# A mixed MLA and mLSTM trunk: decay rows by DRAM transfers, first loads reordered, output factors by token

## The chip, the cores and the metric

One NeuronCore of a Trainium2 chip runs the kernel. The metric is the device time of one execution in microseconds; lower is better. The engines are named as in the profile: PE (TensorE, matmul), DVE (VectorE), ACT (ScalarE), POOL (GpSimd) and SP (SyncE, which here only issues transfers).

## What is computed

Two layers over 512 tokens of width 1024, float32. Each layer adds half a SwiGLU, a token mixer and half a SwiGLU to the residual, each behind an RMS norm; layer 0 mixes with multi-head latent attention, layer 1 with the mLSTM, which the change is about:

```python
def mlstm(h, w_in, b_if, conv_w, conv_b, out_norm, w_o):
    p = h @ w_in
    qk = silu(causal_depthwise_conv(p[..., :QK], conv_w, conv_b))
    ...
    i_pre = gates[..., :H]
    log_f = log_sigmoid(gates[..., H:])
    hid = mlstm_chunkwise(q, k, v, i_pre, log_f)
    hid = hid * rsqrt(mean(hid * hid, axis=-1) + RMS_EPS)
    hid = hid.reshape(B, S, V) * out_norm * sigmoid(o)
    return hid @ w_o
```

Within it, a head's scores are weighted by `exp(D - m_t)`, where `D[t, s] = F[t] - F[s] + i[s]` for s up to t, `F` is the running sum of `log_f` and `m_t` the running maximum that stabilises the exponent. The output of a token is `num / max(|den|, exp(-m_t))`, and then it is normalised over the 128 channels of its head. There are 8 heads.

## The kernel before, in words

Activations lie transposed: channels on the 128 partitions, the 512 tokens along the free axis. A float32 operand is split into a high part (`hi`, rounded by ACT: the CAST rows) and the rest (`lo`, made by DVE), and a product is three matmuls of 128 x 512: hi hi, hi lo, lo hi (`mm3`). Weights come as chunks of 128 x 1024: SP (some on POOL) loads `raw`, ACT casts `whi`, DVE subtracts `wlo`; there are three buffers of each, and `weights()` has the split of the chunk two ahead issued. `defer(n, step)` runs a step when the nth next chunk is asked for. The program is written in this order, but the order within each engine is set by a scheduler that weighs what is ready when; the lists in the section on the change are its outcome.

The program runs the phases f0, a, f1, f2, m, f3 (four feed-forward parts, the attention `a`, the mLSTM `m`).

*Start.* `begin` warms PE with 36 small matmuls, loads the vectors `par`, the constants `cst`, the eight tiles `x` of the residual and the first two chunks of gate and up weights in quarters, and splits them. `stats` squares the x tiles into `acc`; `rstd` sums `acc` over the partitions on PE (`st`), adds a constant on DVE (`ms`), raises to the power -0.5 on POOL (`r`), and `spread(r)` brings it back along the partitions on PE (`bc`).

*mLSTM.* `log_forget` and `stabilise` (run during the first half of `values`) make rows on 8 partitions, one for a head: `m` (the running maximum), `fl` (the running sum within a tile of 128 tokens), `z`, `em` = exp(-m), and `lf` = fl - m. `columns` turns `z` and its shifts to tokens on partitions (bank `cb`, columns `cols`). `decay(h)` needs row h of `lf` on all 128 partitions: before, `spread(rows, h)` did it with a matmul of `rows` (the split of `lf`) against a selector column (L1133), into a PSUM bank. ACT then takes ten exponentials of 128 x 128 (`dw`, L1155), four of which read `dg`, the row with the causal mask added by DVE. The scores `s` times `dw` give the weights `ws[h]`; their sums over s are kept too. `mix(h)` multiplies them with the values (`num`), and adds, in the bank `rows` of `acc`, the sums over s to row h and, through `squares`, the sum of num squared to row 32 + h.

`factors(half, squares)` makes the output factors of four heads. Before, it worked on rows of 512 tokens, 8 partitions: `Abs` and a copy on ACT, three operations on DVE (L1223 to L1225), then PE turned the result to tokens on partitions (`ab`, L1049 by way of `turn`), ACT copied it (`fc`), POOL took `pow(-0.5)` (`fp`), PE turned it back (`fb`), and the split `frows` was spread again for `gated(h)`. It is a generator: its three steps are deferred so that they fall between weight chunks. In the first half they run before the chunk of `conv(3)` and before the first and third chunk of `values(1)`; in the second half between the output projections `out(0, 1)` to `out(0, 3)`, whose matmuls are named `y`.

Of the kernel before, what the change touches and what calls it, by code (L numbers as in the profile page):

```python
# [26 lines left out]
F32 = mybir.dt.float32  # L27
# [39 lines left out]
class Trunk:  # L67
# [68 lines left out]
    def load_pieces(self):  # L136

        name, pieces, pool, plus = self.loads[len(self.loaded)]

        ap = self.row(*name)  # L140
        raw = self.duo(pool, F32) if pool else self.wp.tile([P, W], F32, name="raw", tag="raw")
        self.loaded.append(raw)
        for a, b in pieces:
            queue = self.nc.gpsimd if plus and name[0] == "wgs" else self.nc.sync
            queue.dma_start(out=raw[:, a:b], in_=ap[:, a:b])
            yield
        if plus:
            self.nc.gpsimd.dma_start(out=raw, in_=self.row(*plus), accum_op=ALU.add)  # L148
# [185 lines left out]
    def begin(self, gcol):  # L334
        nc = self.nc
        self.used = 0
        self.later = []
        self.mhalf = self.const.tile([P, NT], F32, name="mhalf")
        nc.vector.memset(self.mhalf, -0.5)

        warm = self.small.tile([P, P], BF16, name="warm", tag="warm", bufs=1)
        nc.vector.memset(warm, 0.0)
        nc.scalar.copy(out=warm[:, 0:1], in_=warm[:, 1:2])
        idle = self.ps2.tile([P, T], F32, name="idle", tag="st")
        for i in range(WARM):
            nc.tensor.matmul(idle[:, 0:P], warm, warm, start=True, stop=True)
        self.par = self.const.tile([P, V_END], F32, name="par")
        nc.sync.dma_start(out=self.par, in_=self.t["vecs"])
        cst = self.const.tile([P, self.t["cst"].shape[1]], F32, name="cst")
        self.ident = cst[:, 0:P]  # L350
        self.mask = cst[:, P:2 * P]
        self.maskT = cst[:, 2 * P:3 * P]
        self.invf, self.sign, self.one = (cst[:, 3 * P + i:3 * P + i + 1] for i in range(3))
        self.sel = cst[:, 3 * P + 3:3 * P + 11]
        self.norm_begin(gcol)
        quarters = [(k * 256, k * 256 + 256) for k in range(4)]
        for i in range(2):
            self.loads[i] = self.loads[i][0], quarters, None, None
        for i in range(2):
            load, split = self.load_pieces(), self.split_pieces(quarters, False)  # L360
            for k in range(4):
                d = 4 * i + k
                nc.sync.dma_start(out=self.x[d], in_=self.t["xT"][d * P:(d + 1) * P, :])
                next(load)
                self.norm_split(d)
                next(split)
            list(load), list(split)
            if i == 0:
                nc.sync.dma_start(out=cst, in_=self.t["cst"])
        self.todo = list(range(ND))  # L370

    def constants(self):
# [614 lines left out]
    def mlstm(self, next_gain):  # L987
# [63 lines left out]
        def small(name, n=32):  # L1051
            return self.small.tile([P, n], F32, name=name, tag=name, bufs=1)
# [28 lines left out]
            v.scalar_tensor_tensor(out=f, in0=pl, scalar=-2.0, in1=f, op0=ALU.mult, op1=ALU.add)  # L1081

        m, fl = self.t512("m"), self.t512("fl")
        rows, frows = self.pair()
        em = self.small.tile([P, T], F32, name="em", tag="rb", bufs=2)

        def stabilise():
            lb = self.bank("lb")
            for j in range(NT):
                turn(lb, j * P, f[:, 8 * j:8 * j + 8])  # L1090
            lf = self.t512("lf")
            s.copy(out=lf[g8], in_=lb[g8])

            ones = self.t512("first")
            v.tensor_tensor_scan(m[g8], lf[g8], z[g8], 0.0, ALU.add, ALU.max)
            nc.gpsimd.memset(ones[g8], 1.0)
            nc.gpsimd.memset(tiles(ones[g8])[:, :, 0:1], 0.0)
            v.tensor_tensor_scan(fl[g8], ones[g8], lf[g8], 0.0, ALU.mult, ALU.add)

            for a in (rows, frows):  # L1100
                nc.gpsimd.memset(a.bitcast(F32), 0.0)
            v.tensor_tensor(out=lf[g8], in0=fl[g8], in1=m[g8], op=ALU.subtract)
            self.split_to((rows[g8], rows[32:40]), lf[g8])
            v.tensor_tensor(out=z[g8], in0=z[g8], in1=fl[g8], op=ALU.subtract)
            v.tensor_scalar(em[g8], m[g8], -1.0, 43.0, ALU.mult, ALU.min)
            s.activation(em[g8], em[g8], AF.Exp)
# [2 lines left out]
        self.defer(4, stabilise)  # L1109
        values(0)  # L1110
        place = [(0, 0), (1, 0), (2, 0), (1, 384)]
        ws, sums, nums, ys, sg, sg_of, acc, which = {}, {}, {}, {}, {}, {}, {}, {}
        cols = small("cols", 80)

        def columns():

            cb = self.bank("cb")
            for i in range(NT):
                src = z[g8, i * P:(i + 1) * P]
                bt = self.t512("bt") if i < NT - 1 else None  # L1120
                for j in range(i, NT):
# [3 lines left out]
                        src = dst  # L1125
                    which[i, j] = 8 * len(which)
                    turn(cb, which[i, j], src)
            s.copy(out=cols, in_=cb[:, 0:80])


        def spread(rows, h):
            b = self.ps2.tile([P, T], F32, name="spread", tag="st")
            nc.tensor.matmul(b, self.selr[:, h:h + 1].broadcast_to([P, P]), rows, start=True, stop=True)  # L1133
            return b

        def decay(h):
            q, k = qk[h // 2], qk[4 + h // 2][h % 2]
            br = spread(rows, h)
            banks = [self.bank("s") for _ in range(3)]
            for i in range(NT):  # L1140
                b, c = place[i]
# [73 lines left out]
        def factors(half, squares):  # L1215

            for f in squares:
                f()
            a, n = self.t512("a"), self.t512("n")
            s.activation(a[g8], acc["rows"][g8], AF.Abs)  # L1220
            sq = self.t512("sq")
            s.copy(out=sq[g8], in_=acc["rows"][32:40])
            v.tensor_tensor(out=a[g8], in0=a[g8], in1=em[g8], op=ALU.max)  # L1223
            v.scalar_tensor_tensor(out=n[g8], in0=a[g8], scalar=EPS, in1=a[g8], op0=ALU.mult, op1=ALU.mult)
            v.scalar_tensor_tensor(out=a[g8], in0=sq[g8], scalar=1.0 / P, in1=n[g8],  # L1225
                                   op0=ALU.mult, op1=ALU.add)
            yield
            ab = self.bank("ab")
            for j in range(NT):
                turn(ab, 8 * j, a[g8, j * P:(j + 1) * P])  # L1230
            fc, fp = small("fc", 16), small("fp", 16)
            s.copy(out=tiles(fc), in_=tiles(ab[:, 0:32])[:, :, 4 * half:4 * half + 4])
            nc.gpsimd.tensor_tensor(out=fp, in0=fc, in1=self.mhalf[:, 0:1].broadcast_to([P, 16]), op=ALU.pow)
            yield
            fb = self.bank("fb")
            for j in range(NT):
                turn(fb, j * P, fp[:, 4 * j:4 * j + 4])
            self.split_to((frows[0:4], frows[32:36]), fb[0:4])
            yield
# [16 lines left out]

        gate(0)
        columns()
        gate(1)
        decay(0)  # L1260
        conv(1)
        decay(1)
        for p in range(3):
            a, b = 2 * p, 2 * p + 1
            conv(p + 5) if p < 2 else gate(5)
            gate(a + 2)
            pending = [mix(a), mix(b)]
            if p == 1:
                steps = factors(0, pending)
                for i in (1, 2, 4):  # L1270
                    self.defer(i, lambda: next(steps))
                conv(3)
                values(1)
# [218 lines left out]
```

## Time and profile before

| | |
|---|---|
| median of 3 runs | 1839.35 us (1837.66 to 1840.27) |
| the profiled execution | 1836.03 us |
| its span in the trace | 1834.3 us |
| PE busy | 1808.8 us, 99% |
| DVE, ACT, POOL busy | 1458.8, 938.6, 181.3 us |
| mLSTM phase | from about 1239 to 1490 us of the span |

Busy shares are averages over stages with different limits. Matmuls are pipelined and their ends modelled, so PE's pace is read from the distance between their starts. A row of the timeline gives the start, the busy time, the engine, line, operation and tiles of a run of like instructions, and in brackets how long the engine had been idle and what ended that.

### The profile page before, as it was taken

Reading aid. Unit: us, or ns where it says so; the run is one execution under the profiler, and the core shown is the slowest. Engines: PE = TensorE matmul, PEld = TensorE weight load, DVE = VectorE, ACT = ScalarE, POOL = GpSimd, SP = SyncE. Lnnn points to the kernel's source line nnn. Section 1 sums busy time; section 2 is a strip of 40 time slices with the busy share of each in tenths; the row PEclk is TensorE's granted clock in tenths of the full one; section 3 lists DMA queues with packets and bytes.
Section 4 is the critical chain, followed back from the end, with each engine's and each line's share of the span. In section 5 each row is a group of like instructions: output and inputs, shape, how many; then the busy total and the mean of one; then the engine's idle time right before and its main releaser. Section 6 shows DMA issues by size and latency. Waiting matters only on the chain.

```text
span 1834.3 us, 30137 instructions
## 1 busy us (share of the span) xinstructions
PE 1808.8 (99%) x12258; PEld 1662.9 (91%) x12258; DVE 1458.8 (80%) x1934; ACT 938.6 (51%) x1350; POOL 181.3 (10%) x233
## 2 busy tenths in 40 slices
PE   9999999999999999999999999999999999999997
PEld 7999989978887999989989999997877779999897
DVE  7887898777767887877797879778878778788875
ACT  5544535567543444534544444455767544445344
POOL 1210001000001210000021000100010012100011
PEclk9999999999999999999999999999999999999999
DMA  8875376421126865466589356633212268753763
GB/s 273 241 221 152 120 189 150 138 75 64 47 94 196 234 190 149 137 184 152 196 217 265 105 162 190 167 106 112 81 63 70 74 186 249 202 151 117 188 150 104
DMA packets 80860, 282.45 MB, mean 154 GB/s; under 512 B 9105, under 2 KB 12305, under 8 KB 80721
## 3 DMA queue, kind: packets, MB, share of 16 engines
q1 hardware_dynamic: 52416, 179.06, 28.2%
q0 software_dynamic: 27728, 100.94, 25.4%
q8 instruction: 96, 1.57, 0.3%
q10 hardware_dynamic: 576, 0.52, 0.1%
q14 instruction: 44, 0.35, 0.1%
HBM read 270.01 MB, written 10.49 MB: 153 GB/s over the span
## 4 chain that ended last, share of the span: by engine, by line
PE 72%; issue 16%; DVE 4%; DMA 3%; ACT 3%; POOL 1%; SPq 0%; POOLq 0%; DVEq 0%; ACTq 0%
PE pz L481 4%; PE pw L479 4%; PE pz L479 4%; PE pw L480 4%; PE pz L480 4%; PE pw L481 4%; PE px L479 4%; PE px L480 4%; PE px L481 4%; PE y L217 3%; PE y L218 3%; PE y L219 3%; DMA sum<-in_wds 2%; PE py L479 2%; PE py L480 2%
## 5 line engine op out<-in xcount | busy, mean ns | idle before, releaser
L185 ACT CAST whi<-raw 128x1024 fp32r<-128x1024 f32 (+1 forms) x278 | 284.4, 1024 | 388.9 <-issue 120.7
L186 DVE TENSOR_TENSOR wlo<-raw,whi 128x1024 fp32r<-128x1024 f32 (+1 forms) x278 | 330.3, 1191 | 110.4 <-ACT whi L185 110.2
L185 ACT CAST whi<-sum 128x1024 fp32r<-128x1024 f32 x208 | 217.4, 1048 | 290.9 <-PE pz L480 72.9
L186 DVE TENSOR_TENSOR wlo<-sum,whi 128x1024 fp32r<-128x1024 f32 x208 | 253.1, 1221 | 67.4 <-ACT whi L185 67.2
L173 DVE TENSOR_TENSOR sum<-raw,sum 128x1024 f32<-128x1024 f32 x88 | 107.3, 1219 | 15.3 <-DMA raw<-in_wgs 14.6
L148 POOL DMA_DIRECT2D sum<-in_wgs x72 | 63.4, 880 | 290.1 <-DMA sum<-in_wgs 273.3
L481 PE MATMUL pz<-b5h,wlo 128*128 128x256 f32 x288 | 81.2, 282 | 0.6 <-DVE wlo L186 0.6
L479 PE MATMUL pz<-b5h,whi 128*128 128x256 f32 x288 | 81.3, 282 | 0.0
L479 PE MATMUL px<-b1h,whi 128*128 128x256 f32 x288 | 81.3, 282 | 0.0
L479 PE MATMUL pw<-b7h,whi 128*128 128x256 f32 x288 | 81.3, 282 | 0.0
L479 PE MATMUL px<-b2h,whi 128*128 128x256 f32 x288 | 81.3, 282 | 0.0
L480 PE MATMUL pw<-b4l,whi 128*128 128x256 f32 x288 | 81.3, 282 | 0.0
L480 PE MATMUL py<-b6l,whi 128*128 128x256 f32 x288 | 81.3, 282 | 0.0
L480 PE MATMUL px<-b1l,whi 128*128 128x256 f32 x288 | 81.3, 282 | 0.0
L479 PE MATMUL py<-b6h,whi 128*128 128x256 f32 x288 | 81.3, 282 | 0.0
L479 PE MATMUL pw<-b4h,whi 128*128 128x256 f32 x288 | 81.3, 282 | 0.0
L479 PE MATMUL pz<-b3h,whi 128*128 128x256 f32 x288 | 81.3, 282 | 0.0
L480 PE MATMUL pz<-b3l,whi 128*128 128x256 f32 x288 | 81.3, 282 | 0.0
L480 PE MATMUL pw<-b7l,whi 128*128 128x256 f32 x288 | 81.3, 282 | 0.0
L480 PE MATMUL px<-b2l,whi 128*128 128x256 f32 x288 | 81.3, 282 | 0.0
L480 PE MATMUL pz<-b5l,whi 128*128 128x256 f32 x288 | 81.3, 282 | 0.0
L481 PE MATMUL pz<-b3h,wlo 128*128 128x256 f32 x288 | 81.2, 282 | 0.0
(423 smaller groups left out, 6201.1 us busy)
## 6 DMA issues: line engine op xcount, KB each, us to landing
sum<-in_wgs POOLq DMA_DIRECT2D x144, 512.0 KB, 6.7
raw<-in_wgs SPq DMA_DIRECT2D x108, 512.0 KB, 5.6
sum<-in_wds POOLq DMA_DIRECT2D x48, 512.0 KB, 6.3
raw<-in_wds SPq DMA_DIRECT2D x48, 512.0 KB, 3.3
sum<-in_wds SPq DMA_DIRECT2D x32, 512.0 KB, 4.4
raw<-in_wgc SPq DMA_DIRECT2D x30, 512.0 KB, 3.6
raw<-in_wdn SPq DMA_DIRECT2D x24, 512.0 KB, 3.7
away<-x SPq DMA_DIRECT2D x16, 512.0 KB, 3.8
```

What stands on the lines that cost most here:

```text
L148: self.nc.gpsimd.dma_start(out=raw, in_=self.row(*plus), accum_op=ALU.add)
L173: self.nc.vector.tensor_tensor(out=t, in0=a, in1=b, op=ALU.add)
L185: self.nc.scalar.copy(out=hi[:, a:b], in_=raw[:, a:b])
L186: self.nc.vector.tensor_tensor(out=lo[:, a:b], in0=raw[:, a:b], in1=hi[:, a:b].bitcast(F32), op=ALU.subtract)
L217: mm(out, lhs[0], rhs[0], start=start, stop=False)
L218: mm(out, lhs[0], rhs[1], start=False, stop=False)
L219: mm(out, lhs[1], rhs[0], start=False, stop=stop)
L479: mm(out, wh, bh[:, b], start=first and e + k == 0, stop=False, skip_group_check=True)
L480: mm(out, wh, bl[:, b], start=False, stop=False, skip_group_check=True)
L481: mm(out, wl, bh[:, b], start=False, stop=last and e + k == 4, skip_group_check=True)
```

## The change

It has three parts. (1) `stabilise` writes `lf` to a DRAM tile `away`, and `apart(p)` brings two rows of it back, each repeated along the 128 partitions by a transfer that POOL issues; `decay` reads that SBUF tile, and the spread by matmul and the split of `lf` go. (2) `begin` issues the loads of the x tiles and the weight quarters alternately and `cst` after them; four memsets of one column on the x tiles stand ahead. (3) `factors` copies rows 0 to 39 of the bank at once (`both`), turns them, and does the arithmetic with tokens on partitions, in 16 columns; `columns` turns `em` too, so that its columns are at hand; the steps of the first half are deferred to the chunks 2, 3 and 5 instead of 1, 2 and 4. The line of `queue` in `load_pieces` is moved out of a loop and issues the same.

```diff
--- before.py
+++ after.py
@@ -136,12 +136,11 @@
     def load_pieces(self):
 
         name, pieces, pool, plus = self.loads[len(self.loaded)]
-
+        queue = self.nc.gpsimd if plus and name[0] == "wgs" else self.nc.sync
         ap = self.row(*name)
         raw = self.duo(pool, F32) if pool else self.wp.tile([P, W], F32, name="raw", tag="raw")
         self.loaded.append(raw)
         for a, b in pieces:
-            queue = self.nc.gpsimd if plus and name[0] == "wgs" else self.nc.sync
             queue.dma_start(out=raw[:, a:b], in_=ap[:, a:b])
             yield
         if plus:
@@ -354,19 +353,23 @@
         self.sel = cst[:, 3 * P + 3:3 * P + 11]
         self.norm_begin(gcol)
         quarters = [(k * 256, k * 256 + 256) for k in range(4)]
+
+        for a in self.xt:
+            nc.vector.memset(a[:, 0:1], 0.0)
         for i in range(2):
             self.loads[i] = self.loads[i][0], quarters, None, None
-        for i in range(2):
-            load, split = self.load_pieces(), self.split_pieces(quarters, False)
-            for k in range(4):
-                d = 4 * i + k
+            load = self.load_pieces()
+            for d in range(4 * i, 4 * i + 4):
                 nc.sync.dma_start(out=self.x[d], in_=self.t["xT"][d * P:(d + 1) * P, :])
                 next(load)
-                self.norm_split(d)
+            list(load)
+        for i in range(2):
+            split = self.split_pieces(quarters, False)
+            for k in range(4):
+                self.norm_split(4 * i + k)
                 next(split)
-            list(load), list(split)
-            if i == 0:
-                nc.sync.dma_start(out=cst, in_=self.t["cst"])
+            list(split)
+        nc.sync.dma_start(out=cst, in_=self.t["cst"])
         self.todo = list(range(ND))
 
     def constants(self):
@@ -1081,7 +1084,8 @@
             v.scalar_tensor_tensor(out=f, in0=pl, scalar=-2.0, in1=f, op0=ALU.mult, op1=ALU.add)
 
         m, fl = self.t512("m"), self.t512("fl")
-        rows, frows = self.pair()
+        frows = self.duo("frows")[:, :T]
+        away = self.dram.tile([8, T], F32, name="rows", tag="rows", bufs=1)
         em = self.small.tile([P, T], F32, name="em", tag="rb", bufs=2)
 
         def stabilise():
@@ -1097,10 +1101,9 @@
             nc.gpsimd.memset(tiles(ones[g8])[:, :, 0:1], 0.0)
             v.tensor_tensor_scan(fl[g8], ones[g8], lf[g8], 0.0, ALU.mult, ALU.add)
 
-            for a in (rows, frows):
-                nc.gpsimd.memset(a.bitcast(F32), 0.0)
+            nc.gpsimd.memset(frows.bitcast(F32), 0.0)
             v.tensor_tensor(out=lf[g8], in0=fl[g8], in1=m[g8], op=ALU.subtract)
-            self.split_to((rows[g8], rows[32:40]), lf[g8])
+            nc.sync.dma_start(out=away, in_=lf[g8])
             v.tensor_tensor(out=z[g8], in0=z[g8], in1=fl[g8], op=ALU.subtract)
             v.tensor_scalar(em[g8], m[g8], -1.0, 43.0, ALU.mult, ALU.min)
             s.activation(em[g8], em[g8], AF.Exp)
@@ -1109,8 +1112,9 @@
         self.defer(4, stabilise)
         values(0)
         place = [(0, 0), (1, 0), (2, 0), (1, 384)]
+        brs = {}
         ws, sums, nums, ys, sg, sg_of, acc, which = {}, {}, {}, {}, {}, {}, {}, {}
-        cols = small("cols", 80)
+        cols = small("cols", 112)
 
         def columns():
 
@@ -1125,7 +1129,9 @@
                         src = dst
                     which[i, j] = 8 * len(which)
                     turn(cb, which[i, j], src)
-            s.copy(out=cols, in_=cb[:, 0:80])
+            for j in range(NT):
+                turn(cb, 80 + 8 * j, em[g8, j * P:(j + 1) * P])
+            s.copy(out=cols, in_=cb[:, 0:112])
 
 
         def spread(rows, h):
@@ -1133,9 +1139,16 @@
             nc.tensor.matmul(b, self.selr[:, h:h + 1].broadcast_to([P, P]), rows, start=True, stop=True)
             return b
 
+        def apart(p):
+
+            both = self.duo("rows", F32)
+            brs[2 * p], brs[2 * p + 1] = both[:, :T], both[:, T:]
+            for h in (2 * p, 2 * p + 1):
+                nc.gpsimd.dma_start(out=brs[h], in_=away[h:h + 1, :].broadcast_to([P, T]))
+
         def decay(h):
             q, k = qk[h // 2], qk[4 + h // 2][h % 2]
-            br = spread(rows, h)
+            br = brs.pop(h)
             banks = [self.bank("s") for _ in range(3)]
             for i in range(NT):
                 b, c = place[i]
@@ -1216,20 +1229,20 @@
 
             for f in squares:
                 f()
-            a, n = self.t512("a"), self.t512("n")
-            s.activation(a[g8], acc["rows"][g8], AF.Abs)
-            sq = self.t512("sq")
-            s.copy(out=sq[g8], in_=acc["rows"][32:40])
-            v.tensor_tensor(out=a[g8], in0=a[g8], in1=em[g8], op=ALU.max)
-            v.scalar_tensor_tensor(out=n[g8], in0=a[g8], scalar=EPS, in1=a[g8], op0=ALU.mult, op1=ALU.mult)
-            v.scalar_tensor_tensor(out=a[g8], in0=sq[g8], scalar=1.0 / P, in1=n[g8],
-                                   op0=ALU.mult, op1=ALU.add)
+            both = self.t512("both")
+            s.copy(out=both[0:40], in_=acc["rows"][0:40])
             yield
             ab = self.bank("ab")
             for j in range(NT):
-                turn(ab, 8 * j, a[g8, j * P:(j + 1) * P])
-            fc, fp = small("fc", 16), small("fp", 16)
-            s.copy(out=tiles(fc), in_=tiles(ab[:, 0:32])[:, :, 4 * half:4 * half + 4])
+                turn(ab, 40 * j, both[0:40, j * P:(j + 1) * P])
+            of = lambda t, c: tiles(t)[:, :, c + 4 * half:c + 4 * half + 4]
+            ab = ab[:, 0:160]
+            fa, fc, fp = small("fa", 16), small("fc", 16), small("fp", 16)
+            s.activation(tiles(fa), of(ab, 0), AF.Abs)
+            v.tensor_tensor(out=tiles(fa), in0=tiles(fa), in1=of(cols[:, 80:112], 0), op=ALU.max)
+            v.scalar_tensor_tensor(out=fa, in0=fa, scalar=EPS, in1=fa, op0=ALU.mult, op1=ALU.mult)
+            v.scalar_tensor_tensor(out=tiles(fc), in0=of(ab, 32), scalar=1.0 / P, in1=tiles(fa),
+                                   op0=ALU.mult, op1=ALU.add)
             nc.gpsimd.tensor_tensor(out=fp, in0=fc, in1=self.mhalf[:, 0:1].broadcast_to([P, 16]), op=ALU.pow)
             yield
             fb = self.bank("fb")
@@ -1256,18 +1269,20 @@
 
         gate(0)
         columns()
+        apart(0)
         gate(1)
         decay(0)
         conv(1)
         decay(1)
         for p in range(3):
             a, b = 2 * p, 2 * p + 1
+            apart(p + 1)
             conv(p + 5) if p < 2 else gate(5)
             gate(a + 2)
             pending = [mix(a), mix(b)]
             if p == 1:
                 steps = factors(0, pending)
-                for i in (1, 2, 4):
+                for i in (2, 3, 5):
                     self.defer(i, lambda: next(steps))
                 conv(3)
                 values(1)
```

What follows on the engines, as lists of instructions in their order on the engine.

PE, first half of `factors` before: the end of `conv(3)` (`qk`), the last matmul into the bank `rows`, and the transposes.

```order
L223 MATMUL rows<-pr,pick 128x512
L219 MATMUL qk<-pr,wlo 128x512
L217 MATMUL qk<-pr,whi 128x512
L218 MATMUL qk<-pr,whi 128x512
L219 MATMUL qk<-pr,wlo 128x512
L1049 MATMUL ab<-cst,a 128x8 x4
L217 MATMUL v<-whi,pr 128x512
```

The same place now (`v` are the matmuls of the first chunk of `values(1)`; seventeen of them stand between the last `rows` and `ab`).

```order
L222 MATMUL rows<-pr,pick 128x512 x3
L217 MATMUL v<-wlo,pr 128x512
L218 MATMUL v<-whi,pr 128x512
L216 MATMUL v<-whi,pr 128x512
...
L218 MATMUL v<-whi,pr 128x512
L1052 MATMUL ab<-cst,both 128x40 x4
L216 MATMUL v<-whi,pr 128x512
```

The transposes have moved from the end of `conv(3)` to the end of the first chunk of `values(1)`. In the second half `ab` keeps its place: eight `y` matmuls follow the last `rows` in both lists.

ACT at the same place before: the factors stand ahead of the silu of `conv(3)`.

```order
L1179 ACT_TABLE_LOAD
L1179 ACTIVATE sg<-sg 128x512
L1220 ACTIVATE a<-rows 8x512
L1222 COPY sq<-rows 8x512
L185 CAST whi<-raw 128x1024
L1232 COPY fc<-ab 128x16
L1011 ACT_TABLE_LOAD
L1011 ACTIVATE conv<-conv 128x512
```

And now: the first exponential of head 4, the `Abs` of the factors and the silu of `conv(3)` follow each other, with a table load at each change of function.

```order
L1192 ACT_TABLE_LOAD
L1192 ACTIVATE sg<-sg 128x512
L228 CAST pr<-sq 128x512 x2
L184 CAST whi<-raw 128x1024 x2
L1233 COPY both<-rows 40x512
L1168 ACT_TABLE_LOAD
L1168 ACTIVATE dw<-rows,cols 128x128
L1241 ACTIVATE fa<-ab 128x16
L184 CAST whi<-raw 128x1024
L1014 ACT_TABLE_LOAD
L1014 ACTIVATE conv<-conv 128x512
L1168 ACT_TABLE_LOAD
```

Exponentials of a head that waited for PE's spread are now placed where ACT is free of other work; the whole list holds 28 table loads, before 22.

SP at the start of the program before.

```order
L348 DMA par<-in_vecs 128x111
L363 DMA x<-in_xT 128x512
L145 DMA raw<-in_wgc 128x256
L363 DMA x<-in_xT 128x512
L145 DMA raw<-in_wgc 128x256 x3
L369 DMA cst<-in_cst 128x395
L363 DMA x<-in_xT 128x512 x2
L145 DMA raw<-in_wgc 128x256 x4
L145 DMA raw<-in_wgc 128x1024
```

Now the pair of an x tile and a quarter comes eight times in turn (the list shows the last two pairs), and `cst` behind them.

```order
L363 DMA x<-in_xT 128x512
L144 DMA raw<-in_wgc 128x256
L363 DMA x<-in_xT 128x512
L144 DMA raw<-in_wgc 128x256
L372 DMA cst<-in_cst 128x395
L144 DMA raw<-in_wgc 128x1024 x3
```

The third x tile has moved from behind three quarters and `cst` to the place behind the second quarter; `cst` and the first 128 x 1024 chunk have moved behind all x tiles.

## Rows read from the trace of the kernel before

**Rows 1.** The page, busy time by engine.

```profile
PE 1808.8 (99%) x12258; PEld 1662.9 (91%) x12258; DVE 1458.8 (80%) x1934; ACT 938.6 (51%) x1350; POOL 181.3 (10%) x233
```

**Rows 2.** PE's waits, whole span: waiter, waited for, us in total, times, longest.

```profile
PE ab L1049 <- DVE a L1225: 3.9, 2, 2.4
...
PE g L217 <- ACT pr L232: 0.9, 1, 0.9
...
PE g L217 <- ACT whi L185: 0.4, 1, 0.4
```

**Rows 3.** Timeline of PE behind the first `ab`: start, busy us, instruction, idle before.

```profile
1358.12 0.41 PE L1049 MATMUL ab<-cst,a 8*128 8x8 f32 x4 [2.37 <-DVE a L1225]
...
1359.43 0.63 PE L217 MATMUL v<-whi,pr 128*128 128x512 f32 x1
...
1361.99 0.61 PE L217 MATMUL v<-whi,pr 128*128 128x512 f32 x1
```

**Rows 4.** Timeline of PE ahead of the second `ab`.

```profile
1435.69 0.40 PE L223 MATMUL rows<-pr,pick 128*128 128x512 f32 x1
...
1437.57 0.39 PE L219 MATMUL y<-pr,wlo 128*128 128x512 f32 x1
1439.48 0.38 PE L1049 MATMUL ab<-cst,a 8*128 8x8 f32 x4 [1.52 <-DVE a L1225]
```

**Rows 5.** Windows, one behind each `ab`: busy by engine, granted clock, DMA share, GB/s.

```profile
1360.00:1361.00 1.00, 1.00 (x4) 0.80 (x3) 0.96 (x2) 0.03 (x1) 1.00 (x1) 0.50 0.11 29
...
1442.00:1443.00 1.00, 1.00 (x4) 0.81 (x3) 0.00 (x0) 0.00 (x0) 1.00 (x1) 0.50 0.90 348
```

**Rows 6.** Timeline of ACT and DVE ahead of the second `ab`.

```profile
1436.12 0.59 ACT L1220 ACTIVATE a<-rows 8x512 f32<-8x512 f32 x1 [2.30 <-PE rows L223]
...
1438.67 0.67 DVE L1225 SCALAR_TENSOR_TENSOR a<-sq,n 8x512 f32<-8x512 f32 x1
1439.27 1.21 DVE L186 TENSOR_TENSOR wlo<-raw,whi 128x1024 fp32r<-128x1024 f32 x1
```

**Rows 7.** The tile `fp`, POOL's power: ns min/median/max, first and last start.

```profile
L1233 POOL TENSOR_TENSOR fp<-fc,mhalf x2: 3028/3615/4202, 1358.9 to 1440.2; 128x16 f32<-128x16 f32 x2
```

**Rows 8.** Timeline of PE, the first `fb`.

```profile
1371.32 0.60 PE L1049 MATMUL fb<-cst,fp 128*4 128x128 f32 x4
```

**Rows 9.** The tile `spread`: ns min/median/max, first and last start.

```profile
L1133 PE MATMUL spread<-pr,selr x16: 391/394/495, 1291.7 to 1453.8; 128*128 128x512 f32 x16
```

**Rows 10.** The tile `pos`, one row sent to 128 partitions by POOL.

```profile
DMA to landing us min/median/max: 6.8/6.8/6.8
```

**Rows 11.** Timeline of DVE and ACT ahead of the first exponentials.

```profile
1278.50 0.68 DVE L1102 TENSOR_TENSOR lf<-fl,m 8x512 f32<-8x512 f32 x1
...
1292.64 0.62 ACT L1179 ACTIVATE sg<-sg 128x512 f32<-128x512 f32 x1
1293.27 1.28 ACT L1155 ACT_TABLE_LOAD   x1
1294.57 0.40 ACT L1155 ACTIVATE dw<-dg,cols 128x128 f32<-128x128 f32 x1
```

**Rows 12.** The page, transfers to DRAM: count, KB each, us to landing.

```profile
away<-x SPq DMA_DIRECT2D x16, 512.0 KB, 3.8
```

**Rows 13.** Window of the first four decays: busy PE, PEld, DVE, ACT, POOL.

```profile
1300.00:1347.00 47.00, 46.69 (x221) 38.48 (x220) 44.14 (x73) 37.73 (x73) 2.25 (x4) 1.00 0.21 68
```

**Rows 14.** Line 1155, the exponentials: ns min/median/max.

```profile
L1155 ACT ACTIVATE dw<-spread,cols x48: 347/367/387, 1294.9 to 1425.6; 128x128 f32<-128x128 f32 x48
L1155 ACT ACTIVATE dw<-dg,cols x32: 399/407/428, 1294.6 to 1425.9; 128x128 f32<-128x128 f32 x32
```

**Rows 15.** Timeline of ACT at the start.

```profile
4.05 0.72 ACT L232 ACTIVATE pr<-x,par 128x512 fp32r<-128x512 f32 x1 [1.82 <-DMA x<-in_xT]
4.68 0.39 ACT L185 CAST whi<-raw 128x256 fp32r<-128x256 f32 x1
4.97 0.63 ACT L287 ACTIVATE acc<-x 128x512 f32<-128x512 f32 x1
```

## The prediction

> **What bounds the kernel now.** I read the profile in this order: busy shares, PE's waits by line, then the timeline around the longest waits. TensorE (PE) is busy 99% of the span [rows 1], so a time is won here only where PE does fewer matmuls, waits less, or runs at a higher clock. The list of PE's waits [rows 2] is led by one line of the mLSTM, the transposes `ab` in `factors`: 3.9 us in two waits. Two waits at the start of the program, for `pr` and `whi` of the first tiles, follow with 0.9 and 0.4 us.
>
> The waits at `ab` cost more than the list says. On PE's timeline [rows 3] the first `ab` had waited 2.37 us; then the matmuls from 1359.43 to 1361.99 start (1361.99 - 1359.43) / 6 = 0.427 us apart, while 128x512 matmuls in the stage otherwise start 0.235 us apart (eight of them from 1435.69 to 1437.57 [rows 4]). The granted clock is 0.50 there, the lower level of 1.2 GHz, and it is 0.50 again after the second `ab` [rows 5], which had waited 1.52 us. About eight matmuls are slow each time: 8 x (0.427 - 0.235) = 1.5 us.
>
> Why does PE wait there? The chain behind the second wait is an `Abs` on ACT from 1436.12 and then three DVE operations and an unrelated one, the last starting at 1438.67 and taking 0.67 [rows 6]; eight matmuls of cover end at 1437.80.
>
> **The change, part by part.**
>
> *Factors.* One ACT copy of 40 rows (about the 0.59 us of the `Abs` [rows 6], which reads the same bank) is now all that stands between the last `rows` matmul and `ab`. In the first half the transposes also move one weight chunk later: 17 matmuls, 17 x 0.235 = 4.0 us, lie between the last `rows` and `ab`, where four did. In the second half eight still lie there: the copy ends at 1436.12 + 0.59 = 1436.71, PE arrives at 1437.80, 1.1 us to spare. I take both waits as gone. Each cost its idle time and 0.16 of refilling (1439.48 - 1437.80 = 1.68 for an idle of 1.52 [rows 4]): 2.53 + 1.68 = 4.2 us. With the waits go both slow stretches, 2 x 1.5 = **3.1 us**. Together **-7.3**.
>
> Next in line is `fb`, which needs the `pow` on POOL. In the second half 24 matmuls (5.6 us) stand between `ab` and `fb`, and the path between them grows: `Abs` behind a 128x1024 cast, then three DVE operations behind a 128x1024 `wlo` of 1.21 [rows 6], then `pow`, which took 3.0 us in one half and 4.2 in the other [rows 7]. Measured from `ab`: 0.4 for the transposes, 0.9 until the cast is out of the way and `Abs` done, 1.2 for `wlo`, 0.4 for three small operations as an estimate, and 3.0 to 4.2 makes 5.9 to 7.1 against PE's 6.0. So PE waits 0 to 1.1 there; I take **+0.3**. The first half has 48 matmuls there, 11 us.
>
> The transposes turn 40 rows instead of 8. Four `ab` of 8 columns take 0.41 [rows 3], four `fb` of 128 columns 0.60 [rows 8], so eight of 40 cost 0 to 0.4 us more; four of `em` in `columns` cost about 4 x 0.07. I take **+0.4**.
>
> *Decay rows.* Eight `spread` matmuls go (the sixteen of that line include eight for `frows`, which stay [rows 9]): 8 x 0.235 = **-1.9**. In their place `lf` goes to DRAM and comes back as eight transfers of one row to 128 partitions, issued by POOL. The trace has one like it, `pos`: 6.8 us to landing [rows 10]. `lf` is made at 1278.50 + 0.68 [rows 11]; with 3.8 for the way to DRAM, the median for `away` [rows 12], and 6.8 back, rows 0 and 1 are there at about 1290 and 1291; the first exponential started at 1294.57 [rows 11]. Later rows have one whole iteration. I cost the transfers at nothing; without that cover PE would still have until `num` of head 0, after the matmuls of three weight chunks. SP holds its next weight load until `lf` is there, some 3 us, against weights cast two chunks (11 us) ahead: nothing.
>
> What the rows in SBUF do change is ACT's order. With no wait for PE, the exponentials of a head are placed earlier, between sigmoids and silus, so the function table is swapped more often: the order holds 28 table loads where it held 22. A load costs 1294.57 - 1293.27 = 1.30 us of ACT [rows 11]. Four of the extra loads lie between 1300 and 1347, where ACT is busy 37.7 of 47 us and DVE 44.1 [rows 13]; and 24 exponentials there now read SBUF at 0.41 instead of PSUM at 0.37 [rows 14], 1.0 more. ACT rises to 37.7 + 5.2 + 1.0 = 43.9 of 47: it fits, tightly. PE's order allows for it: `num` of head 3 is spread among the `qk` matmuls of the next convolution, 11 x 0.235 = 2.6 us later. Against that, decays no longer wait for PE, and head 4's exponentials fall into the idle stretch of `values(1)`. I take **0**, with -2 and +2.6 as ends.
>
> *Start.* The x tiles and weight quarters now come alternately; the waits of 0.9 and 0.4 (1.7 with refill) go if x tile 2, so far behind three quarters and `cst`, lands in turn. But `cst` and the four 128x1024 chunks come after all of them, and ACT's and DVE's queues pack tighter. ACT needs per tile 0.63 (`pr`) + 0.29 (`whi`) + 0.6 (square) [rows 15], for eight tiles 12.2 us from 4.05, with the casts of `cst` and waits for data some 1.4 more: it begins the first 128x1024 cast at about 17.7 and ends it at 18.7, where PE, undelayed, has done its 48 matmuls by about 18.0. That is a wait of 0 to 1.2; I take 0.5. Then `ms`, the head of the rstd chain, stands on DVE behind two `wlo` instead of ahead of one: 1.2 later [rows 6], of which I let 0.9 reach PE at `bc`. Sum -1.7 + 0.5 + 0.9 = **-0.3**, ends -1.7 and +1.
>
> **The sum:** -7.3 + 0.3 + 0.4 - 1.9 + 0 - 0.3 = -8.8 us. The profiled execution took 1836.03 us, 3.3 under the median of the runs, 1839.35; I take the sum off the median: **1830.5 us**.
>
> **The rivals.**
>
> *The wait moves to `fb`.* If `pow` takes 4.2 in the second half, PE waits up to 1.1 there and the clock may fall as after the 1.52: 0.8 + 1.5 more than forecast, 1832.8. For: the count of 24 matmuls. Against: one of the two took only 3.0, and the ends were added up as if nothing overlapped.
>
> *ACT becomes the bound (slower than before).* In the two pairs before the first `ab`, ACT's and DVE's idle time may be waiting, not room. Then the six loads, 7.8, and the 48 dearer exponentials, 1.9, reach PE in full at the `num` matmuls, with one slow stretch of 1.5: +11.2, 1841.7. It decides once more than 8.8 us arrive; for it speaks DVE at 94% between 1300 and 1347, against it that weights are cast two chunks ahead and `num` was moved.
>
> *A table swap that costs twice as much.* A load may also have to wait until ACT has run dry. The trace has such a place: the load at 1293.27 starts 0.63 after the start of the sigmoid before it, which took 0.62, and holds ACT 1.30 in all [rows 11], so little of that is to be seen. If each of the six cost twice the 1.30, the rival above would become 1841.7 + 7.8 = 1849.5. The Trainium skill says this on its page "ScalarE: Activation LUTs", section "What ACT_TABLE_LOAD costs": a load of about 1283 ns and a drain of about 1380 ns, 2.66 us for each switch. The trace agrees with the load (1283 ns) and shows no such drain.
>
> **How the numbers follow.** Forecast 75% (its own range 1826.5 to 1834: the ends of start and decays), `fb` 15%, ACT 8%, the dear swap 2%. The range 1825 to 1837.5 adds the `fb` case with a full wait and part of the ACT case; it leaves out the rest of ACT and the dear swap. A measurement can tell about 0.2% here, 3.7 us. Faster means under 1835.7: the forecast but for its tail, and nearly all of `fb`: 85%. The same 7%, from the tails of these and a mild ACT case. Slower 8%.
>
> **What would show it.** No PE wait at `ab` above 0.3 us and a granted clock of 1.00 through 1355 to 1365 and 1437 to 1447; eight `spread` matmuls, not sixteen; transfers of the rows landing within 8 us and no ACT or DVE wait on them. At the start, waits for `pr` gone, and small ones at the first `g` of the third chunk and at `bc`. The prediction is wrong if PE waits more than 2 us in all at `num`, `rows` or `s` between 1300 and 1360, or if the clock still falls near `fb`.

## The result, and the profile after

The changed kernel takes **1810.07 us** (median of 4 runs, 1807.55 to 1811.88), the kernel before 1838.51 in the same session: ratio 0.9844, 95% interval 0.9827 to 0.9861. That is 28.4 us less, where 8.8 were forecast, and far below the range of 1825 to 1837.5. The profiled execution took 1807.55 us, the shortest of the four; its span is 1805.8. Of one kernel further down (the changed one with a distance of 192), one of six executions took 3163.77 us at a granted clock of 0.758, and its median is that of the other five.

The page, busy time by engine [rows 1]:

```profile
PE 1778.9 (99%) x12254; PEld 1632.3 (90%) x12254; DVE 1451.3 (80%) x1937; ACT 946.1 (52%) x1353; POOL 185.0 (10%) x240
```

PE is still busy 99%, and only 4 of its matmuls fewer ran, but its busy time fell by 30 us. PE's waits after the change, the same view as [rows 2]:

```profile
PE py L484 <- DVE wlo L185: 3.9, 2, 2.1
...
PE pz L484 <- DVE wlo L185: 2.1, 6, 0.5
PE dw L626 <- DVE wlo L185: 1.4, 3, 0.5
PE dv L626 <- DVE wlo L185: 1.3, 2, 0.8
...
PE rows L222 <- ACT pr L228: 0.3, 1, 0.3
```

`ab`, `pr` and `whi` of the start are gone from the list. In their place stand 8.7 us of waits for `wlo` (1.5 before), in the feed-forward phases that the change does not touch.

**What came as forecast.** Behind `ab` and `fb` (timeline of PE after the change, [rows 3, 8]) there is no wait, and the granted clock stays at 1.00 (windows after the change, against 0.50 in [rows 5]):

```profile
1346.26 0.40 PE L218 MATMUL v<-whi,pr 128*128 128x512 f32 x1
1346.59 0.44 PE L1052 MATMUL ab<-cst,both 40*128 40x40 f32 x4
...
1358.26 0.60 PE L1052 MATMUL fb<-cst,fp 128*4 128x128 f32 x4
```

```profile
1346.00:1350.00 4.00, 4.00 (x20) 3.01 (x19) 3.19 (x7) 2.91 (x4) 1.71 (x1) 1.00 0.46 132
...
1432.00:1436.00 4.00, 4.00 (x19) 3.22 (x18) 2.39 (x5) 1.50 (x3) 0.00 (x0) 1.00 0.41 135
```

**What the forecast did not have.** Windows of PE, 700 to 750 us and others: busy time with the number of matmuls, granted clock, DMA share, GB/s. First the kernel before, then the changed one:

```profile
700.00:750.00 50.00, 50.00 (x419) 1.00 0.60 172
...
1050.00:1100.00 50.00, 50.00 (x419) 1.00 0.55 158
```

```profile
700.00:750.00 50.00, 50.00 (x431) 1.00 0.56 160
950.00:1000.00 50.00, 50.00 (x427) 1.00 0.90 256
1050.00:1100.00 50.00, 50.00 (x431) 1.00 0.46 145
```

All of these are 128x256 matmuls of the feed-forward phases, without a wait and at the same granted clock of 1.00. A window counts every matmul that touches it, so their distance is the window plus one matmul's 0.28 us, divided by the count: 50.28 / 419 = 120.0 ns before, 50.28 / 431 = 116.7 ns now, and 117.8 in one stretch. Some 8,900 such matmuls are in the trace. This is where the time went. By all start-to-start distances of PE in the two traces:

| PE, us between starts | before | changed | |
|---|---|---|---|
| 128x256 matmuls without a wait behind them | 1074.3 | 1048.0 | -26.3 |
| 128x256 matmuls with a wait behind them, the wait included | 5.8 | 15.4 | +9.6 |
| all else (128x512, small matmuls, mLSTM, start) | 745.4 | 733.2 | -12.2 |

The third line is the part that the forecast speaks of; the first and the second are not in it at all.

### The profile page after: what moved, and what is told of

It is laid out like the page before. It is cut to its first block, busy times and chain, and to the rows that moved or that the text cites. A ratio compares the mean times of both kernels' runs of the same rounds, so it can differ in the third digit from the quotient of the medians.

```text
span 1805.8 us, 30166 instructions
## 1 busy us (share of the span) xinstructions
PE 1778.9 (99%) x12254; PEld 1632.3 (90%) x12254; DVE 1451.3 (80%) x1937; ACT 946.1 (52%) x1353; POOL 185.0 (10%) x240
## 3 DMA queue, kind: packets, MB, share of 16 engines
q0 software_dynamic: 28368, 103.04, 26.3%
## 4 chain that ended last, share of the span: by engine, by line
PE 73%; issue 16%; DVE 5%; DMA 3%; ACT 2%; POOL 1%; SPq 0%; POOLq 0%; DVEq 0%; ACTq 0%
PE pz L484 4%; PE pw L482 3%; PE pw L483 3%; PE pw L484 3%; PE pz L482 3%; PE pz L483 3%; PE px L482 3%; PE px L484 3%; PE px L483 3%; PE y L216 3%; PE y L217 3%; PE y L218 3%; DVE wlo L185 2%; PE py L482 2%; PE py L484 2%
## 5 line engine op out<-in xcount | busy, mean ns | idle before, releaser
L184 ACT CAST whi<-raw 128x1024 fp32r<-128x1024 f32 (+1 forms) x278 | 284.5, 1024 | 355.6 <-issue 106.7
L484 PE MATMUL py<-b6h,wlo 128*128 128x256 f32 x288 | 80.7, 280 | 3.9 <-DVE wlo L185 3.9
L484 PE MATMUL px<-b1h,wlo 128*128 128x256 f32 x288 | 80.4, 279 | 0.0
L484 PE MATMUL pw<-b7h,wlo 128*128 128x256 f32 x288 | 80.4, 279 | 0.0
L484 PE MATMUL pw<-b4h,wlo 128*128 128x256 f32 x288 | 80.4, 279 | 0.0
L484 PE MATMUL px<-b2h,wlo 128*128 128x256 f32 x288 | 80.4, 279 | 0.0
```

What stands on the lines that cost most here:

```text
L184: self.nc.scalar.copy(out=hi[:, a:b], in_=raw[:, a:b])
L484: mm(out, wl, bh[:, b], start=False, stop=last and e + k == 4, skip_group_check=True)
```

## The experiments

**What sets the pace?** In the program, the pool `wp` (the weights' tiles) starts at byte 20320 of each partition and `arena` (the moving operands of most matmuls) at 83648. The pool `small` lies between. The change makes its tile `cols` 32 columns wider and adds `fa` of 16, (32 + 16) x 4 = 192 bytes, so the arena starts at 83840. I call *distance* the arena's start less that of `wp`, modulo 256 bytes: 96 before, 32 now. Theory PLACE says that this sets the pace, theory PROGRAM that the new order of work or transfers does. A pad, unused columns that widen a tile, pushes on whatever lies behind it: 48 columns in the kernel before move the arena (and two small tiles, `fc` and `fp`); the order of all instructions stays.

```diff
-        cols = small("cols", 80)
+        cols = small("cols", 128)[:, :80]
```

> The kernel before, with the arena (the pool that holds the matmuls' moving operands) 192 bytes further on in each partition, at the place where the changed kernel has it; the order of all instructions is that of before. Theory PLACE (the pace of the 128x256 matmuls depends on where the arena lies): they start 116.7 ns apart, not 120.0; 8736 of them x 3.33 = 29 us less, given back in part by new waits for wlo of some 5 to 7 us, as in the changed kernel: 1814 to 1818 us. Theory PROGRAM (the pace comes from the reordered start, transfers or instructions of the change): 120.0 ns and 1838.5 us, as before.

The other way round, the changed kernel with 16 columns of pad, so that the distance is 96 again:

```diff
-        cols = small("cols", 112)
+        cols = small("cols", 128)[:, :112]
```

> The changed kernel with the arena 64 bytes further on, so that its distance from a multiple of 128 and of 256 bytes is that of before. PLACE, if the distance from a multiple of 128 decides: 128x256 matmuls 120.0 ns apart, and the time is that of the change without the new pace: by the forecast 1838.5 - 8.8 = 1830 us (1825 to 1837). PLACE with another modulus: 116.7 and some 1810 us. PROGRAM: 116.7 ns and 1810 us.

Windows of PE, first of the kernel before with 192 bytes, then of the changed kernel with 64:

```profile
700.00:750.00 50.00, 50.00 (x426) 1.00 0.56 161
1050.00:1100.00 50.00, 50.00 (x431) 1.00 0.55 164
```

```profile
700.00:750.00 50.00, 50.00 (x419) 1.00 0.59 172
1050.00:1100.00 50.00, 50.00 (x419) 1.00 0.56 159
```

PROGRAM falls as the cause of the pace: this went with the 192 bytes, and came back to 120.0 ns with the old distance. The times (the changed program at 32 is that of the result, where the kernel before took 1838.51; the rest are of one later session):

| us, ratio to before with interval | distance 96 | distance 32 |
|---|---|---|
| program before | 1838.89 | 1821.71, 0.9899 (0.9883 to 0.9916) |
| changed program | 1827.94, 0.9935 (0.9919 to 0.9950) | 1810.07, 0.9844 (0.9827 to 0.9861) |

The place gives -17.2 in one program and -17.9 in the other, the program -10.9 at one place and -11.6 at the other: they add up. The first run came out 3.7 us above the upper end that PLACE expected; in its profile about half of the stretches ran at 117.8 ns.

**Which distance?** Two more pads of the kernel before (16 and 32 columns) and four of the changed one (8, 24, 40 and 56), each run once, with the same edit:

> The kernel before with the arena 64 bytes further on. PLACE with a modulus of 128: as the 192 bytes, 116.7 ns and 1814 to 1818 us. PLACE with a larger modulus: 120.0 or a third level. PROGRAM: 120.0 ns, 1838.5 us.

> The kernel before with the arena 128 bytes further on. PLACE with a modulus of 128: 120.0 ns, 1838.5 us, as before. PLACE with a larger modulus: may be another level. PROGRAM: 120.0 ns, 1838.5 us.

> The changed kernel, arena 32 bytes further on: its distance from the weights' tiles is 64 bytes past a multiple of 256 (the change has 32, the kernel before 96, the run with the arena 192 bytes on 32, those with 64 and 128 bytes 160 and 224). If the distance sets the pace in fine steps: between the 116.7 of 32 and the 120.0 of 96, or one of the two. Time by its pace: 1810 us at 116.7, 1819 at 118.3, 1828 at 120.0.

> The changed kernel, arena 96 bytes further on: distance 128 past a multiple of 256. No run has it; between 96 (120.0) and 160 (117.3 to 118.7). 1814 to 1828 us by the pace.

> The changed kernel, arena 160 bytes further on: distance 192 past a multiple of 256, between 160 (117.3 to 118.7) and 224 (118.3). 1814 to 1822 us by the pace.

> The changed kernel, arena 224 bytes further on: distance 0 past a multiple of 256, between 224 (118.3) and 32 (116.7). 1808 to 1820 us by the pace; a level under 116.7 would show a place better than the change's.

The first two took 1835.59 and 1834.64 us, the other four 1804.73, 1820.49, **1788.80** and 1814.38 (the kernel before took 1843.97 once in the session of these four). The expectation of small steps between neighbours failed: 1788.80 lies far below its 1814 to 1822, and 1804.73 below its 1810 to 1828. Mean distance of starts, by distance of the pools, with the runs below included:

| distance | kernels | 128x256, ns | 128x512, ns |
|---|---|---|---|
| 0 | changed +224 | 120.0 | 227 |
| 32 | changed; before +192 | 116.7 or 117.8 | 233.3 |
| 64 | changed +32 | 117.8, seldom 113.3 | 229 |
| 96 | before; changed +64; single parts | 120.0 | 233.3 |
| 128 | changed +96 | 118.7 to 120.0 | 232.4 to 233.4 |
| 160 | before +64 | 117.3 to 118.7 | 234.3 |
| 192 | changed +160; before +96 | 113.3 or 117.8 | 233.3 |
| 224 | before +128 | 118.3 | 233.4 |

A modulus of 128 falls: the kernel before gave 120.0 without a pad and 118.3 with 128 bytes. Distance 96 occurs 256 bytes apart (arena at 83648 and at 83904) with the same 120.0, and 192 (83744 and 84000) with the same two levels.

**Distance, or the arena's own place?** A pad in `const`, the pool ahead of `wp`, moves both. In the kernel before both move by 64 bytes; in the changed one `wp` by 64 and the arena by 224:

```diff
-        self.mhalf = self.const.tile([P, NT], F32, name="mhalf")
+        self.mhalf = self.const.tile([P, 20], F32, name="mhalf")[:, :NT]
```

> The kernel before with everything from the pool const on, so the weights' tiles wp and the arena, 64 bytes further on; their distance is that of before, and the arena lies where the run with 64 bytes had it. If the distance between weights and arena sets the pace: 120.0 ns throughout and some 1838 us. If the arena's own place does: the mixed 117 to 119 ns of the run with 64 bytes.

> The changed kernel with weights' tiles 64 and arena 224 bytes further on: the distance is 192 past a multiple of 256, and the arena lies where the run with 224 bytes had it (120.0 ns and 227 ns for 128x512 there, 1814 us). If the distance decides: 113.3 ns, 233.3 ns for 128x512, 1786 to 1792 us. If the arena's own place does: 120.0 and 227 ns, 1814 us.

Windows of PE. The kernel before, first with the arena alone moved by 64 bytes (distance 160), then with both moved (the arena at the same byte, distance 96):

```profile
700.00:750.00 50.00, 50.00 (x424) 1.00 0.57 170
```

```profile
700.00:750.00 50.00, 50.00 (x419) 1.00 0.56 165
```

The changed kernel, first with the arena moved by 224 bytes and `wp` at its old place (distance 0), then with `wp` moved too (distance 192):

```profile
528.00:553.00 25.00, 25.00 (x112) 1.00 0.54 189
625.00:650.00 25.00, 25.00 (x210) 1.00 0.93 259
700.00:750.00 50.00, 50.00 (x419) 1.00 0.56 158
```

```profile
528.00:553.00 25.00, 25.00 (x109) 1.00 0.54 189
625.00:650.00 25.00, 25.00 (x223) 1.00 0.97 278
700.00:750.00 50.00, 50.00 (x427) 1.00 0.58 172
```

In the last two fences the first window holds 128x512 matmuls: (25 + 0.40) / 112 = 227 ns against 233. With the arena at the same byte, both widths changed their pace when `wp` moved; with the distance kept, the pace stayed at 120.0. The distance decides. The run of the kernel before with both moved took 1853.11 us, run once, against some 1838 expected: it has 7.5 us of waits for `wlo` at `py` against none before, and the granted clock fell to 0.50 in three stretches of the feed-forward phases (at 124, 1020 and 1218 us). By the starts its waits are 10.0 us longer in all and these stretches cost some 5.6, of the 17.0 by which its span is longer; why the weights came late there stays open. That of the changed kernel took 1801.03, above its 1786 to 1792; over half of it ran at 117.8.

Two levels at one distance are two states of the same stream. Timeline of PE in the changed kernel at distance 192 (the run of 1788.80 us), around a wait:

```profile
286.45 0.28 PE L625 MATMUL dz<-b5l,whi 128*128 128x256 f32 x1
...
288.38 0.28 PE L624 MATMUL dv<-b3h,whi 128*128 128x256 f32 x1
...
289.17 0.39 PE L626 MATMUL dv<-b3h,wlo 128*128 128x256 f32 x1 [0.40 <-DVE wlo L185]
...
289.63 0.28 PE L626 MATMUL dv<-b3h,wlo 128*128 128x256 f32 x1
...
291.87 0.28 PE L624 MATMUL dx<-b1h,whi 128*128 128x256 f32 x1
```

Seventeen distances ahead of the wait: (288.38 - 286.45) / 17 = 113.5 ns. Nineteen behind it: (291.87 - 289.63) / 19 = 117.9 ns; over longer stretches the two levels are 113.3 and 117.8. A level stays until some later wait, or until a delay too short to be listed as one: in the second profile at distance 192 it goes from 113.3 to 117.8 where two starts at 697.01 us lie 0.15 us apart. Which state follows I could not tell.

**The place without the change, and the best place.** The kernel before with 24 columns of pad (distance 192); the changed kernel at distance 192 (the run of 1788.80 us) again, now with six executions; and a version with a distance of its own for each width, by moving the weights of all 128x512 matmuls 48 columns within wider tiles:

```diff
+        o = 0 if name[0] in ("st", "dn") else 48
-        hi = self.wp.tile([P, W], F32R, name="whi", tag="whi")
+        hi = self.wp.tile([P, W + 64], F32R, name="whi", tag="whi")[:, o:o + W]
...
-        cols = small("cols", 112)
+        cols = small("cols", 152)[:, :112]
```

(`lo` likewise.)

> The kernel before, order untouched, with the arena 96 bytes further on: distance from the weights' tiles 192 past a multiple of 256, as in the changed kernel with the arena 160 bytes on. If the distance alone sets the pace: 113.3 ns in place of 120.0, 8736 x 6.7 = 58 us less, given back in part by waits for weights (12 to 16 us there): 1790 to 1800 us, below the changed kernel's 1810 without one instruction of the change. If the program has a share in the pace: 120.0 and 1838 us, or another level.

> The changed kernel with the arena 160 bytes further on (distance 192), now timed: 1786 to 1793 us, after 1788.8 in the single look; a ratio to the kernel before of some 0.973.

> The changed kernel with the arena at distance 192 for the weights of the 128x256 matmuls, and the weights of all 128x512 matmuls moved by 192 bytes within their tiles (64 columns wider), so that these have distance 0. If each width's pace follows the distance of its own operands: 113.3 ns and 227 ns; some 2500 matmuls x 6.4 ns = 16 us less than with distance 192 for all, less new waits: 1772 to 1782 us. If the pace of 128x512 comes from elsewhere: 233.3 ns and 1789 us.

The kernel before, not one instruction moved: 1812.30 us, ratio 0.9845 (0.9815 to 0.9875), the same as the whole change, though 12 us above the 1790 to 1800 I expected; half of it ran at 117.8. The changed kernel at distance 192: 1794.45, 0.9756 (0.9730 to 0.9781), just above its 1786 to 1793. With a distance for each width: **1789.10 us**, 0.9723 (0.9699 to 0.9746). It beats the kernel before and the change, but it missed its 1772 to 1782, and its gain over distance 192 for all, 5.4 us, is not clear of the two intervals. What shows that each width follows its own distance is the pace: the windows have the 128x512 matmuls at 227 ns, and both states of the 128x256 ones, more often the slow one:

```profile
528.00:553.00 25.00, 25.00 (x112) 1.00 0.53 185
...
700.00:750.00 50.00, 50.00 (x444) 1.00 0.56 169
1050.00:1100.00 50.00, 50.00 (x427) 1.00 0.41 137
```

**The parts of the change alone,** each at distance 96, where no pace changes. Their edits are the hunks of the diff: for the factors those of `columns`, `factors` and the chunks 2, 3 and 5 (with `cols` 128 wide, which moves the arena by 256 bytes); for the rows those with `away` and `apart`; for the start that of `begin`.

> The kernel before with the new factors alone (one copy of 40 rows, arithmetic with tokens on partitions, the steps at the chunks 2, 3 and 5), and with the arena 256 bytes further on, where the matmuls should keep the 120.0 ns of before. Forecast: waits and slow clock at ab go (-7.3), fb +0.3, larger transposes +0.4: -6.6, some 1832 us. Rival (the factors explain all that the change brought at that pace): -11, 1828 us. Rival (waits only move): 1836 to 1839 us.

> The kernel before with the decay rows by transfers from DRAM alone; all tiles lie where they lay before (120.0 ns). Forecast: eight spread matmuls less, -1.9, and nothing else: 1837 us. Rival (ACT becomes late from more table loads): 1839 to 1846 us. Rival (decays that no longer wait for PE also remove waits for s, num and og): -4 to -6, 1833 to 1835 us.

> The kernel before with the reordered start alone; all tiles lie where they lay before (120.0 ns). Forecast: -0.3, ends -1.7 and +1: 1838 us. The profile of the changed kernel with the pace of before shows the first px 2.2 us earlier: by that 1836 us.

| | us, ratio with interval | mLSTM, first `gates` to the next phase's first `bc` | first `px` |
|---|---|---|---|
| before | 1839.29 | 252.1 | 55.7 |
| factors alone | 1834.00, 0.9970 (0.9954 to 0.9986) | 245.3 | 55.1 |
| rows alone | 1839.73, 0.9999 (0.9987 to 1.0010) | 252.0 | 55.3 |
| start alone | 1837.30, 0.9987 (0.9976 to 0.9997) | 252.2 | 54.3 |
| all, distance 96 | 1827.94, 0.9935 (0.9919 to 0.9950) | 240.9 | 53.5 |
| the change | 1810.07 | 240.6 | 54.5 |

The factors do what was forecast: 6.8 us in the mLSTM, 5.3 (2.6 to 8.5) in the time. The rows alone give nothing, though eight matmuls went. PE's waits of that run, and ACT ahead of its first `ab`:

```profile
PE ab L1049 <- DVE a L1233: 6.2, 2, 4.6
```

```profile
1339.26 1.28 ACT L1011 ACT_TABLE_LOAD   x1
...
1341.21 1.28 ACT L1163 ACT_TABLE_LOAD   x1
...
1346.57 1.28 ACT L1011 ACT_TABLE_LOAD   x1
...
1353.07 1.28 ACT L1187 ACT_TABLE_LOAD   x1
...
1357.83 0.58 ACT L1228 ACTIVATE a<-rows 8x512 f32<-8x512 f32 x1
```

Four table loads in 15 us (two in the same place before), and the old factors stand behind them: the first `ab` waits 4.64 us, where it was 2.37 [rows 3]. I read that as the rival in which ACT becomes the bound; a part of it stands on DVE, where two `wlo` of 2.36 us in all now precede the first operation of the factors. In the change the new factors take the place of that wait, so the rows are worth 245.3 - 240.9 = 4.4 us once the factors are there (the start alone leaves the mLSTM at 252.2).

## Why the prediction was wrong

**The step that failed** is the second sentence: that at 99% busy "a time is won here only where PE does fewer matmuls, waits less, or runs at a higher clock". There is a fourth way: the same matmuls, at the same granted clock, closer together. The sum -8.8 left everything outside the start and the mLSTM at its old pace; no term and no rival had a place for 192 bytes of tiles in a pool ahead of the arena, and of its signs of being wrong none came. Distance 32 gave -17.9 at the median; in the profiled executions that is 26.3 us of pace less 9.6 of new waits.

The Trainium skill says on its page "TensorE: Matmul & The Clock Gate", section "Step-by-step: what each phase is for", that PE reads the streaming operand and the weights through two independent ports and that loading the next weights takes no read bandwidth from the running matmul. By that alone, the place of one operand against the other should not matter; here it changed the distance of the matmuls' starts, 113.3 to 120.0 ns. That the two reads get in each other's way is the reading at hand, but no run here shows that they do, or where.

**The terms that the forecast had,** at distance 96, came to -10.9 against -8.8. That these lie so close is in part luck: each part alone gives -5.3, +0.4 and -2.0, some 4 us less than all together, since the rows pay only once the factors are there. Term by term:

- *`ab` and the slow clock, -7.3; `fb`, +0.3; larger transposes, +0.4.* Right: no wait at `ab` or `fb`, clock 1.00, and -6.8 in the mLSTM for the factors alone against -6.6. The +0.3 of `fb` did not come: POOL's `pow` took 3.9 us in one half and 2.9 in the other, and the matmuls between covered it.
- *Decay rows, -1.9 and 0 for ACT's order.* Eight matmuls went, and the transfers landed in time. Of the ACT term, with ends of -2 and +2.6, the lower one came: the mLSTM lost some 2.5 us more (252.1 - 6.8 - 1.9 = 243.4 without it, 240.9 with all parts). Of these 2.5, 1.7 are PE's waits there: 2.8 us with the factors alone, 1.1 with all parts, as those at `og` and `s` are gone and those at `rows` shorter. Tile `spread`, and the landing of the row transfers after the change [rows 9, 10]:

```profile
L1139 PE MATMUL spread<-frows,selr x8: 390/392/502, 1364.3 to 1428.4; 128*128 128x512 f32 x8
```

```profile
DMA to landing us min/median/max: 3.5/4.2/4.7
```

- *Start, -0.3.* Too small: the first `px` came 1.4 us earlier with the start alone, whose time fell by 2.0 (0.6 to 4.4), 2.2 with all parts at distance 96 and 1.2 in the changed kernel; it also moved by 0.4 to 0.6 with the factors or the rows alone, which leave the start as it was. Of the two losses in that term one came. Timelines of ACT, DVE and PE at the start [rows 15]:

```profile
17.15 1.98 ACT L184 CAST whi<-raw 128x1024 fp32r<-128x1024 f32 x2
```

```profile
18.89 2.35 DVE L185 TENSOR_TENSOR wlo<-raw,whi 128x1024 fp32r<-128x1024 f32 x2
21.16 0.15 DVE L306 TENSOR_SCALAR ms<-st 128x4 f32<-128x4 f32 x1
```

```profile
24.59 0.47 PE L324 MATMUL bc<-diag,onesr 128*128 128x512 f32 x1 [0.67 <-DVE diag L320]
```

  `ms` stands behind two `wlo` and `bc` waits 0.67 us (0.24 before), where 0.9 more was put in. The large cast began at 17.15, not 17.7, and no `g` waited for it, where 0.5 was put in.

**The rivals.** The wait did not move to `fb`. ACT late from table loads is seen, but only with the old factors. The dear table swap is not to be seen: the loads above hold ACT 1.28 us each.

**Where the pace was given back.** A faster PE uses up its weights sooner. Chain of waits in the changed kernel at 656 us, and the wait that it ends in:

```profile
647.01 0.03 DVE slab L489
647.04 7.88 DMA raw<-in_wgs
...
655.01 1.23 DVE sum L172
...
656.84 0.52 DVE wlo L185
```

```profile
658.03 0.39 PE L484 MATMUL py<-b6h,wlo 128*128 128x256 f32 x1 [1.81 <-DVE wlo L185]
```

A load starts when DVE frees a buffer, takes 7.9 us, and `sum` and `wlo` follow: PE waits. At distance 192 these waits grow further (in the run of 1788.80 us `dv` 3.7 and 3.4 us, `pz` 2.7, `wlo` or `whi` late each time), and there they cost the clock too, which they did not in the change. Windows of PE in that run, behind waits of 1.56 and 1.40 us at `dv`, each soon followed by one of 0.75:

```profile
308.00:310.00 2.00, 2.00 (x11) 0.50 0.00 0
1734.00:1736.00 2.00, 2.00 (x11) 0.50 0.03 8
```

So the loads and splits of the weights look like the next limit; no run here makes them quicker. The pace need not be the only cause of late weights: the run of 1853.11 us had such waits at 120.0 ns.

## What to carry to other kernels

A change that adds or widens small tiles can move every pool behind them. Before you credit the code, run the old code with a pad that gives the new addresses, and the new code with the old ones: two runs separate place from program. Where matmuls bound the kernel, count them in equal windows before and after; if the count differs at the same granted clock, look at the addresses of both operands, and then try pads on purpose: here one was worth as much as the whole change.

## What the runs showed of the hardware that I had not expected

- The pace of float32r matmuls depended on the distance in SBUF between moving operand and weights, modulo 256 bytes as far as two distances show it: 113.3 to 120.0 ns for 128x256, 227 to 234 ns for 128x512. The best of the eight distances tried differs: 192 for the one, 0 for the other.
- At some distances the stream has two states, 113.3 and 117.8 ns at 192, 116.7 and 117.8 at 32, and it changed at a wait of 0.4 us.
- The clock fell to 0.50 behind waits of 1.52 and 2.37 us at `ab` [rows 4, 5], and behind 1.56 and 1.40 us at `dv` at distance 192 (each with one of 0.75 us soon after), but not behind the 1.81 us at `py` in the changed kernel, nor behind the 2.12 us at its second such wait (at 1562 us):

```profile
658.00:660.00 2.00, 1.97 (x16) 1.00 0.85 166
660.00:662.00 2.00, 1.55 (x13) 1.00 0.02 4
662.00:664.00 2.00, 2.00 (x19) 1.00 0.00 0
```
